# Second half's row sums by quarters, batched first norm, another order of the seven products, activation maximum in four parts

## The chip, the cores and the metric

One core of one Trainium2 chip runs the whole program in one launch. The metric is the device time of that core in microseconds (us); three runs of the kernel before took 2927.37, 2935.06 and 2939.93 us, median 2935.06.

## What is computed

One layer of a decoder trunk on x (1 x 2048 x 1024, float32). Cut to what matters:

```python
mod = silu(c) @ w_ada + b_ada;  sh1, sc1, g1, sh2, sc2, g2 = split(mod, 6)
h  = rms(x, ln1_g) * (1 + sc1) + sh1
u  = h @ w_in                       # q, k, v of 8 FoX heads and 4 differential heads
x  = x + g1 * (concat(fox(u), diff(u)) @ w_out)
h2 = rms(x, ln2_g) * (1 + sc2) + sh2
y  = (silu(h2 @ w_gate) * (h2 @ w_up)) @ w_down      # 1024 -> 2816 -> 1024
x  = x + g2 * y
```

## The kernel before

Every matmul operand is kept as two float16 parts, high and low, and each product is three matmuls (high x high, high x low, low x high). The 2048 rows are 16 blocks of 128.

The program has four stages. First the modulation and the first norm: `first_norm` squares a block on ScalarE with the row sum as accumulator output (L230), makes 1/sqrt with Ln, Exp and three small VectorE operations (`rsqrt`, L126 to L135), and scales the block on GpSimd (L235); `first_hT` turns it with PE transposes and splits it. `first_rows(c)` lists these steps for the four blocks of chunk c, and `run` mixes them by weights with the input projection of the chunk before. Then come the projection and attention of eight head groups. Then `out_proj(blk)` for the 16 blocks, which also stores the new x to `x1d` in DRAM and leaves 1/rms of each row in `r2`.

The last stage is the feed-forward part. It multiplies by a scheme of seven products in place of eight: the rows are taken in pairs of blocks (z) and the 1024 inputs in halves (h), and product i takes one combination of row quarters (`BSUM`), one combination of weight quarters (`ASUM`), and adds its result to the outputs. `norm_row` scales and shifts a row block (two VectorE operations over 1024 columns); `norm_sum` makes one combination (a GpSimd sum over 512 columns where two quarters are involved, a ScalarE copy to the high half, a VectorE subtraction to the low half), and transposes it by DMA. For the first half of the rows (pairs 0 to 3) this is done during the out projection, straight into `comb(i)`. For the second half (pairs 4 to 7) it is done inside the first pass, in iterations 2, 4, 6 and 8: `norm_load` takes two stage buffers for the two rows of a pair, each of the seven sums takes a third, and the transposed result goes to `hcd` in DRAM. There are three stage buffers in all (`stage`, tag S), shared with the down weights.

The loop has 22 iterations q and one more for the last downs: 11 weight chunks of 256 columns of the 2816, once for each half of the rows. An iteration has 14 slots: seven products in `ORDER` for the gate (w = 0), seven for the up weights (w = 1). `product(q, w, i)` is 12 matmuls of 512 columns into a bank of ps_st, ps_pv or ps_mx (2, 2 and 3 banks); products 2 and 3 add onto the banks of 4 and 5. What follows each product on the other engines makes `act`, four parts of 128 x 512, from sums of products, Silu for w = 0, the multiplication for w = 1. `act_scale(q)` takes the maximum over all of act (L123), spreads it over the partitions with a small matmul (`colmax`, L108, on the one bank of ps_ip), and makes a power of two from it; `act_split` then writes `aT`, and 16 `down` of six matmuls each, in the next iteration, multiply it by the down weights and are added to x on VectorE (L1153). Gate and up weights are loaded whole (`gu_load`, 1 MB), bounded by a maximum, summed on GpSimd (L1038) and split; the down weights are loaded, bounded (L1061, L1062) and split (`dn_load`, `dn_scale`, `dn_split`). Each of the four weight and activation maxima of an iteration goes through `colmax` and so puts one small matmul into PE's queue.

The order in which Python emits these steps is a priority; a planner with times of its own puts each engine's instructions into a fixed order from it, and inserts all semaphores. Every engine works its queue in order. All DMAs go over SP's queue. The list `st[slot]` says after which product a step is emitted, and `DOWNAT` how many downs follow each slot's product.

## Time and profile before

| | |
|---|---|
| runs | 2927.37, 2935.06, 2939.93 us |
| profiled execution | 2939.51 us, its span 2937.7 us |
| mean granted clock of TensorE | 0.980 |
| busy: PE, VectorE, ScalarE, GpSimd | 2728.9, 2111.3, 1441.2, 1609.5 us |
| stretch of the feed-forward part in the trace | about 1547 to 2937 us |

PE, DVE, ACT and POOL are TensorE, VectorE, ScalarE and GpSimd, SP is the queue that issues DMAs, L123 is line 123 of the kernel before. The granted clock is given as a share of 2.4 GHz. An idle time in square brackets is the time that the engine stood before that instruction, with what released it.

### The profile page before, as it was taken

The numbers are of one execution on the slowest core, as the hardware profiler recorded it, in microseconds if no ns is written. First come the engines' busy times: TensorE is split into PE (matmuls) and PEld (weight loads), VectorE is DVE, ScalarE is ACT, GpSimd is POOL, SyncE is SP. The second block draws the span as 40 slices with busy tenths as digits, with TensorE's granted clock in tenths as the row PEclk, the third lists the DMA queues.
The fourth block names the chain that finished last, engine by engine and source line by source line (L and its number), as shares of the span: only waits on it lengthen the run. The fifth ranks groups of instructions, "written<-read, shape, count | busy, mean of one in ns | idle before, by whom it ended". The sixth has DMA issues, their size and how long they took to land.

```text
span 2937.7 us, 49384 instructions
## 1 busy us (share of the span) xinstructions
PE 2728.9 (93%) x18902; PEld 1479.9 (50%) x18902; DVE 2111.3 (72%) x4077; ACT 1441.2 (49%) x2725; POOL 1609.5 (55%) x1392
## 2 busy tenths in 40 slices
PE   5789989899999999999989998899999999999998
PEld 3456656566665655664444343444444444444443
DVE  7786675857758686656744887787878778778775
ACT  4666667666676777786543422333323332233230
POOL 2566666665667787675542645444545444535430
PEclk9899999999999999999999999999999999999999
DMA  6232231322224233234776223224234511112101
GB/s 230 77 82 61 63 73 39 82 53 67 73 50 94 53 105 95 49 103 118 171 196 202 85 68 98 72 79 110 70 108 150 165 59 57 58 52 64 58 22 58
DMA packets 269902, 261.92 MB, mean 89 GB/s; under 512 B 204376, under 2 KB 221144, under 8 KB 263904
## 3 DMA queue, kind: packets, MB, share of 16 engines
q1 hardware_dynamic: 269664, 258.75, 31.0%
q8 instruction: 148, 2.42, 0.4%
q14 instruction: 90, 0.74, 0.1%
HBM read 173.55 MB, written 36.91 MB: 72 GB/s over the span
## 4 chain that ended last, share of the span: by engine, by line
PE 52%; DVE 21%; DMA 12%; POOL 6%; ACT 6%; issue 4%; SPq 0%; POOLq 0%; DVEq 0%; ACTq 0%
PE ps_mx L1149 10%; PE ps_ip L437 10%; PE ps_st L1091 7%; PE ps_pv L1091 6%; DMA stg<-in_w_ada_dram 3%; PE ps_ip L934 3%; DMA stg<-stg 2%; PE ps_mx L1091 2%; PE ps_st L579 2%; DVE t_mxc L548 2%; PE ps_st L580 2%; PE ps_pv L609 2%; PE ps_mx L546 2%; PE ps_pv L608 2%; PE ps_pv L607 2%
## 5 line engine op out<-in xcount | busy, mean ns | idle before, releaser
L593 POOL TENSOR_TENSOR pxs<-pxs 128x512 f16<-128x512 f32 (+3 forms) x640 | 683.3, 1082 | 325.8 <-ACT pxs L590 191.8
L1091 PEld LDWEIGHTS <-mt 128*128 128x128 f16 x3696 | 361.8, 99 | 446.7 <-issue 22.0
L437 PE MATMUL ps_ip<-wbuf,ht 128*128 128x384 f16 (+1 forms) x2952 | 560.6, 332 | 26.1 <-DVE vts L144 13.5
L1149 PE MATMUL ps_mx<-wide,ht 128*128 128x512 f16 x2112 | 505.4, 382 | 11.5 <-ACT ht L139 5.6
L1038 POOL TENSOR_TENSOR pxm<-vts 128x512 f32<-128x512 f32 x220 | 295.7, 1370 | 347.1 <-DMA vts<-in_w_gu_dram 316.3
L585 ACT ACTIVATE pxs<-ps_st,cells 128x512 f32<-128x512 f32 (+3 forms) x640 | 388.7, 619 | 142.5 <-PE ps_st L580 68.9
L437 PEld LDWEIGHTS <-ht 128*128 128x128 f16 x3072 | 295.7, 99 | 243.5 <-issue 46.2
L1091 PE MATMUL ps_st<-ht,mt 128*128 128x512 f16 x1584 | 383.0, 386 | 5.6 <-ACT mt L1094 3.2
L1091 PE MATMUL ps_pv<-ht,mt 128*128 128x512 f16 x1584 | 383.3, 380 | 1.1 <-ACT mt L1096 1.1
L590 ACT ACTIVATE pxs<-pxs 128x512 f16<-128x512 f32 (+3 forms) x640 | 350.7, 565 | 16.4 <-PE ps_pv L609 7.6
L607 PE MATMUL ps_pv<-vts,pxs 128*128 128x129 f16 (+1 forms) x2176 | 342.6, 207 | 4.2 <-DVE os L626 3.1
L608 PE MATMUL ps_pv<-vts,pxs 128*128 128x128 f16 (+1 forms) x2176 | 344.7, 208 | 0.0
L1149 PEld LDWEIGHTS <-ht 128*128 128x128 f16 x2112 | 206.3, 98 | 266.7 <-issue 16.9
L609 PE MATMUL ps_pv<-vts,pxs 128*128 128x129 f16 (+1 forms) x2176 | 325.6, 207 | 9.8 <-POOL pxs L593 8.9
L548 DVE TENSOR_REDUCE t_mxc<-ps_mx 128x1 f32<-128x512 f32 x384 | 256.9, 682 | 93.8 <-PE ps_mx L546 92.0
L1153 DVE SCALAR_TENSOR_TENSOR mt<-ps_mx,t_ai,mt 128x512 f32<-128x512 f32 x352 | 256.6, 743 | 75.5 <-PE ps_mx L1149 75.2
L607 PEld LDWEIGHTS <-pxs 128*128 128x128 f16 x2176 | 208.2, 97 | 56.7 <-ACT pxs L585 3.5
L579 PE MATMUL ps_st<-mt 67*128 67x512 f16 (+7 forms) x640 | 223.8, 350 | 10.4 <-ACT pxs L585 10.2
L609 PEld LDWEIGHTS <-pxs 128*128 128x128 f16 x2176 | 206.8, 99 | 50.0 <-POOL pxs L593 24.3
L608 PEld LDWEIGHTS <-pxs 128*128 128x128 f16 x2176 | 208.0, 97 | 35.3 <-issue 4.1
L580 PE MATMUL ps_st<-mt 128*128 128x512 f16 (+3 forms) x640 | 223.8, 350 | 0.0
L546 PE MATMUL ps_mx<-mt 71*128 71x512 f16 (+7 forms) x640 | 197.3, 350 | 19.6 <-DVE t_mxc L548 13.1
(266 smaller groups left out, 4097.0 us busy)
## 6 DMA issues: line engine op xcount, KB each, us to landing
vts<-in_w_gu_dram SPq DMA_DIRECT2D x44, 1024.0 KB
stg<-in_w_down_dram SPq DMA_DIRECT2D x44, 512.0 KB
stg<-in_w_ada_dram SPq DMA_DIRECT2D x32, 512.0 KB
stg<-in_w_in_dram SPq DMA_DIRECT2D x24, 512.0 KB
mt<-in_w_ada_dram SPq DMA_DIRECT2D x16, 512.0 KB
mt<-mt SPq DMA_DIRECT2D x128, 64.0 KB
mixed<-os SPq DMA_DIRECT2D x32, 256.0 KB
stg<-in_w_out_dram SPq DMA_DIRECT2D x16, 512.0 KB
```

The source lines that it names most:

```text
L437: T.matmul(pt[:, 0:N], lhsT=h4[:, k, hs, c : c + P], rhs=w4[k // 4][:, k % 4, ws, 0:N], start=(i == 0), stop=(i == len(terms) - 1))
L548: V.tensor_reduce(out=mx[:, 4 * j + n : 4 * j + n + 1], in_=b[:, 0:w], op=ALU.max, axis=AX.X)
L579: T.matmul(b[:, c0:QC], lhsT=K2[0:K, kb * P : (kb + 1) * P], rhs=QA[0:K, q0:q1], start=True, stop=False, skip_group_check=True)
L585: A.activation(p32[:, c0:QC], b[:, c0:QC], AF.Exp, bias=pshift, scale=1.0)
L590: A.activation(ph[:, c0:QC], p32[:, c0:QC], AF.Copy, bias=0.0, scale=1.0)
L593: (V if hilo[1] == "V" else G).tensor_tensor(out=pl[:, c0:QC], in0=p32[:, c0:QC], in1=ph[:, c0:QC], op=ALU.subtract)
L607: T.matmul(pv[:, jj, :], lhsT=lhs_h, rhs=v4[:, kb, h, 0 : W + 1], start=first, stop=False, skip_group_check=True)
L608: T.matmul(pv[:, jj, 0:W], lhsT=lhs_h, rhs=v4[:, kb, h, W + 2 : 2 * W + 2], start=False, stop=False, skip_group_check=True)
L609: T.matmul(pv[:, jj, :], lhsT=lhs_l, rhs=v4[:, kb, h, 0 : W + 1], start=False, stop=end, skip_group_check=True)
L1038: G.tensor_tensor(out=sums[:, k * 512 : (k + 1) * 512], in0=raw[:, a * 512 : (a + 1) * 512], in1=raw[:, b * 512 : (b + 1) * 512], op=op)
L1091: T.matmul(b.rearrange("p (b n) -> p b n", b=4), lhsT=aw[w][:, APOS[i] * 4 + k, ws, :], rhs=cb[:, :, 2 * k + hb, :], start=(fresh and k == ...
L1149: T.matmul(b, lhsT=aT[:, th, as_, f, j * P : (j + 1) * P], rhs=dnb[:, (2 * q + f) % 4, ws, n * 512 : (n + 1) * 512], start=(f == 0 and z = ...
```

## The change

It has four parts and two that come with them.

The second half's rows and sums become small units: `late_row` loads one block, scales and shifts it and stores it to a new DRAM tile `yd`; `late_sum` loads the one or two quarters that it needs from `yd` into one stage buffer, sums, splits, transposes and stores to `hcd`. Their steps have slots of their own; four units begin in every iteration from 0 to 8.

The first norm of chunks 1 to 3 squares the four blocks one after the other, makes one 1/sqrt of four columns, and scales each block.

The order of the products becomes 6, 4, 5, 1, 2, 3, 7. The sum of products 6 and 1 is made after product 1, and act[1,1] after product 3; after the last product only act[0,0] is left.

The maximum over act is taken in four parts of 512 columns, after the slots that make them, and `act_scale` reduces over the four.

With these, the down weights' steps move to the head of the iteration and the downs two slots later, and the first gate weights' steps are emitted between the out projections of blocks 10 to 13.

```diff
+    def first_stats(c, r4):
+        ss = small(4, "dss", bufs=2)
+        for j in range(4):
+            A.activation(sqs.bitcast(F16), xcs[c][:, j, :], AF.Square, bias=0.0, scale=1.0, accum_out=ss[:, j : j + 1])
+        V.tensor_scalar(out=ss, in0=ss, scalar1=1.0 / D, scalar2=EPS, op0=ALU.mult, op1=ALU.add)
+        r = small(4, "drr", bufs=2)
+        rsqrt(ss, r, 4)
+        r4["r"] = r
...
-        rows = [(0, lambda: hts.append(htile()))]
+        r4 = {}
+        rows = [(0, lambda: hts.append(htile())), (2, lambda: first_stats(c, r4))]
         for j in range(4 * c, 4 * c + 4):
-            rows.append((1, lambda j=j: first_norm(j)))
+            rows.append((0.5, lambda j=j: first_scale(j, r4)))
             rows.append((1, lambda j=j: first_hT(j)))
...
-    ORDER = (4, 5, 1, 2, 3, 7, 6)
+    ORDER = (6, 4, 5, 1, 2, 3, 7)
...
+    def late_row(blk):
+        st = {}
+        def load():
+            st["y"] = stage()
+            nc.sync.dma_start(st["y"], x1d[blk])
+        return [(0, load), (1, lambda: norm_rows2(st["y"], blk)), (2, lambda: nc.sync.dma_start(yd[blk - 8], st["y"]))]
+
+    def late_sum(jj, i):
+        (za, ha), op, other = BSUM[i]
+        st = {}
+        def load():
+            e = st["e"] = stage()
+            for c, (z, h) in enumerate([(za, ha)] + ([other] if other else [])):
+                nc.sync.dma_start(e[:, c * 512 : (c + 1) * 512], yd[2 * jj - 8 + z][:, h * 512 : (h + 1) * 512])
...
+        def add():
+            e = st["e"]
+            if other:
+                G.tensor_tensor(out=e[:, 0:512], in0=e[:, 0:512], in1=e[:, 512:1024], op=op)
+            s3, hi, _, _ = parts()
+            A.activation(hi, s3, AF.Copy, bias=0.0, scale=1.0)
+        def low():
+            s3, hi, lo, _ = parts()
+            V.tensor_tensor(out=lo, in0=s3, in1=hi, op=ALU.subtract)
...
+        return [(0, load), (1, add), (2, low), (3, turn), (4, store)]
...
         elif i == 1:
             V.tensor_tensor(out=tmp, in0=b, in1=s4s, op=ALU.add)
+            V.tensor_tensor(out=s5s, in0=e["b", w, 6], in1=tmp, op=ALU.add)
...
         elif i == 3:
             V.tensor_tensor(out=dif, in0=b, in1=dif, op=ALU.subtract)
+            G.tensor_tensor(out=s5s, in0=s5s, in1=dif, op=ALU.add)
             if w == 0:
                 A.activation(act[:, 1, 0], b, AF.Silu, bias=0.0, scale=gi)
+                A.activation(act[:, 1, 1], s5s, AF.Silu, bias=0.0, scale=gi)
             else:
                 V.tensor_tensor(out=act[:, 1, 0], in0=b, in1=act[:, 1, 0], op=ALU.mult)
+                G.tensor_tensor(out=act[:, 1, 1], in0=s5s, in1=act[:, 1, 1], op=ALU.mult)
         elif i == 7:
...
             V.tensor_tensor(out=tmp, in0=b, in1=tmp, op=ALU.add)
             if w == 0:
-                G.tensor_tensor(out=act[:, 1, 1], in0=tmp, in1=dif, op=ALU.add)
-                A.activation(act[:, 1, 1], act[:, 1, 1], AF.Silu, bias=0.0, scale=gi)
+                A.activation(act[:, 0, 0], tmp, AF.Silu, bias=0.0, scale=gi)
             else:
-                G.tensor_tensor(out=tmp, in0=tmp, in1=dif, op=ALU.add)
-                G.tensor_tensor(out=act[:, 1, 1], in0=tmp, in1=act[:, 1, 1], op=ALU.mult)
+                V.tensor_tensor(out=act[:, 0, 0], in0=tmp, in1=act[:, 0, 0], op=ALU.mult)
...
+    def act_bound(q, th, f):
+        e = sets[q]
+        if (th, f) == (0, 1):
+            e["am4"] = small(4, "am4", bufs=2)
+        k = 2 * th + f
+        V.tensor_reduce(out=e["am4"][:, k : k + 1], in_=act[:, th, f], op=ALU.max, axis=AX.X, apply_absolute_value=True)
...
-        g = colmax(absmax(uhm, BF16), "ip")
+        g = colmax(absmax(e["am4"], BF16), "ip")
...
+    run(outs[10:11])
     gu_bound(0, 0)
...
+    run(outs[11:13])
     gu_scale(0, 0)
+    run(outs[13:14])
...
-    run(outs[10:16])
+    run(outs[14:16])
...
-        return [(0, gu_load, q, 1), (1, gu_bound, q, 1)] + [(1 + k // 2, gu_sum, k) for k in range(5)] + [(2, gu_scale, q, 1)]
+        return [(0, gu_load, q, 1), (1, gu_bound, q, 1)] + [(1 + k // 2, gu_sum, k) for k in range(5)] + [(3, gu_scale, q, 1)]
...
-    DOWNAT = (0, 0, 0, 0, 2, 2, 2, 2, 2, 2, 1, 1, 1, 1)
+    DOWNAT = (0, 0, 0, 0, 0, 1, 2, 2, 2, 2, 2, 2, 2, 1)
...
+    seq = pairs[0] + pairs[1] + lates[0] + pairs[2] + lates[1] + pairs[3] + lates[2] + lates[3]
+    for k, steps in enumerate(seq):
+        for d, f in steps:
+            late[14 * (k // 4) + (5, 6, 10, 11)[k % 4] + d].append(f)
...
             for f in range(2):
-                at(3 + f, dn_load, q, f)
-            at(5, dn_scale, q)
+                at(f, dn_load, q, f)
+                at(1 + f, dn_bound, q, f)
+            at(3, dn_scale, q)
             for f in range(2):
-                at(9 + f, dn_split, q, f)
+                at(4 + f, dn_split, q, f)
+            for k, (th, f) in zip((12, 13, 13), ((0, 1), (1, 0), (1, 1))):
+                at(k, act_bound, q, th, f)
         if q:
-            at(0, act_scale, q - 1)
-            at(1, act_split, q - 1, 0)
-            at(2, act_split, q - 1, 1)
+            at(0, act_bound, q - 1, 0, 0)
+            at(1, act_scale, q - 1)
+            at(2, act_split, q - 1, 0)
+            at(3, act_split, q - 1, 1)
...
-            at(4, gu_scale, q + 1, 0)
+            at(5, gu_scale, q + 1, 0)
```

## Rows read from the trace of the kernel before

**Rows 1.** The page's first part: span; engine, busy us, share, instructions.

```profile
span 2937.7 us, 49384 instructions
PE 2728.9 (93%) x18902; PEld 1479.9 (50%) x18902; DVE 2111.3 (72%) x4077; ACT 1441.2 (49%) x2725; POOL 1609.5 (55%) x1392
```

**Rows 2.** Windows, both passes: stretch, length, PE, PEld, DVE, ACT, POOL busy, clock, DMA.

```profile
1651.00:2227.90 576.90, 534.10 (x2413) 236.98 (x2414) 457.59 (x644) 173.78 (x208) 297.33 (x188) 0.97 0.28 84
2402.80:2856.60 453.80, 453.80 (x2128) 206.40 (x2127) 357.67 (x529) 142.34 (x159) 206.08 (x138) 1.00 0.16 53
```

**Rows 3.** PE's waits, 1651 to 2227.9 us: us in total, times, longest.

```profile
PE ps_ip L108 <- DVE t_amh L123: 28.9, 6, 7.3
...
PE ps_mx L1149 <- DVE mt L1153: 3.0, 3, 2.1
```

**Rows 4.** PE in order of time around one stall: start us, us, instruction.

```profile
2017.17 2.75 PE L1091 MATMUL ps_mx<-ht,mt 128*128 128x512 f16 x12
...
2025.16 5.34 PE L1091 MATMUL ps_pv<-ht,mt 128*128 128x512 f16 x24
2036.48 0.29 PE L108 MATMUL ps_ip<-idb,t_amh 128*128 128x128 bf16 x1 [5.98 <-DVE t_amh L123]
2037.07 4.94 PE L1091 MATMUL ps_st<-ht,mt 128*128 128x512 f16 x12 [0.30 <-DVE pxm L1099]
```

**Rows 5.** VectorE in order of time, the same stall.

```profile
2034.13 2.29 DVE L123 TENSOR_REDUCE t_amh<-uhm 128x1 bf16<-128x2048 f32 x1 [3.59 <-POOL uhm L1126]
```

**Rows 6.** GpSimd in order of time, the same stall.

```profile
2027.49 1.27 POOL L984 TENSOR_TENSOR stg<-stg 128x512 f32<-128x512 f32 x1 [4.50 <-DMA hcd<-stg]
2028.72 1.27 POOL L1125 TENSOR_TENSOR pxm<-pxm,wide 128x512 f32<-128x512 f32 x1
2029.95 2.93 POOL L1038 TENSOR_TENSOR pxm<-vts 128x512 f32<-128x512 f32 x2
2032.85 1.25 POOL L1126 TENSOR_TENSOR uhm<-pxm,uhm 128x512 f32<-128x512 f32 x1
```

**Rows 7.** Window just after that stall, columns as in rows 2.

```profile
2036.80:2041.40 4.60, 4.33 (x11) 1.58 (x11) 3.96 (x6) 0.63 (x1) 0.29 (x1) 0.50 0.00 0
```

**Rows 8.** The last iteration's end, VectorE and PE in order of time.

```profile
2902.84 0.69 DVE L1120 TENSOR_TENSOR pxm<-ps_mx,pxm 128x512 f32<-128x512 f32 x1 [1.84 <-PE ps_mx L1091]
...
2908.59 0.29 PE L108 MATMUL ps_ip<-idb,t_amh 128*128 128x128 bf16 x1 [4.50 <-DVE t_amh L123]
```

**Rows 9.** Groups by line, 1651 to 2227.9 us: busy us, mean ns; idle before.

```profile
L984 POOL TENSOR_TENSOR stg<-stg 128x512 f32<-128x512 f32 x20 | 29.5, 1473 | 103.3 <-DMA hcd<-stg 101.0 <-DVE wide L144 2.4
L989 DVE TENSOR_TENSOR stg<-stg 128x512 f16<-128x512 f32 x28 | 24.6, 880 | 44.5 <-ACT stg L988 44.5
...
L974 DVE SCALAR_TENSOR_TENSOR stg<-stg,cells,vts 128x1024 f32<-128x1024 f32 x8 | 15.4, 1930 | 0.0
L975 DVE TENSOR_TENSOR stg<-stg,vts 128x1024 f32<-128x1024 f32 x8 | 12.8, 1594 | 0.0
```

**Rows 10.** VectorE's reduction over 512 columns, line 455: ns min/median/max.

```profile
L455 DVE TENSOR_REDUCE t_ss<-os x64: 668/676/689, 63.9 to 1331.6; 128x8 f32<-128x512 f32 x64
```

**Rows 11.** PE at the end of the out projection, in order of time.

```profile
1539.86 0.29 PE L108 MATMUL ps_ip<-idb,t_amh 128*128 128x128 bf16 x1 [7.37 <-DVE t_amh L123]
1540.53 6.64 PE L934 MATMUL ps_ip<-mt,wide 128*128 128x512 f16 x24 [0.38 <-DVE t_cm L109]
```

**Rows 12.** PE's waits, 2227.9 to 2860 us.

```profile
PE ps_ip L108 <- DVE t_amh L123: 3.5, 1, 3.5
```

**Rows 13.** First norm: groups by line, ScalarE and VectorE, 40 to 440 us.

```profile
L230 ACT ACTIVATE os<-mt 128x1024 f16<-128x1024 f32 x12 | 12.7, 1055 | 3.2 <-DVE t_ss L455 3.2
...
L230 ACT ACTIVATION_READ_ACCUMULATOR os<-mt 128x1 f32 x12 | 2.3, 188 | 0.0
```

**Rows 14.** VectorE's split by form, second pass, 2402.8 to 2856.6 us.

```profile
L144 DVE SCALAR_TENSOR_TENSOR wide<-stg,t_dws,wide 128x1024 f16<-128x1024 f32 x16 | 29.1, 1856 | 3.9 <-ACT wide L139 3.9
...
L144 DVE SCALAR_TENSOR_TENSOR mt<-vts,t_ws,mt 128x1024 f16<-128x1024 f32 x16 | 20.5, 1283 | 4.0 <-ACT mt L139 3.1
```

More of the change, by code (lines that the diff above doesn't have):

```diff
@@ L292, in first_norm, with first_scale @@
         norm_rows(xt, xt)
+    def first_stats(c, r4):
[6 more added lines that the diff above has]
+        r4["r"] = r
+    def first_scale(blk, r4):
+        xt = xcs[blk // 4][:, blk % 4, :]
+        G.tensor_scalar(out=xt, in0=xt, scalar1=r4["r"][:, blk % 4 : blk % 4 + 1], scalar2=0.0, op0=ALU.mult, op1=ALU.add)
     def first_hT(blk):
@@ L909, in trunk @@
     hcd = dram.tile([7, 4, P, 1024], F16, tag="hcd", name="hcd")
+    yd = dram.tile([8, P, D], F32, tag="yd", name="yd")
     hs = []
@@ L989, in norm_sum, with parts, turn, store @@
         V.tensor_tensor(out=hl[:, :, 1, :], in0=s3, in1=hl[:, :, 0, :], op=ALU.subtract)
-        row = hl.rearrange("p k s n -> p (k s n)")
-        if jj < 4:
-            nc.sync.dma_start(comb(i)[:, jj], row, transpose=True)
-        else:
-            tr = e[:, 0:512].bitcast(F16)
-            nc.sync.dma_start(tr.rearrange("p (k n) -> p k n", n=P), row, transpose=True)
-            nc.sync.dma_start(hcd[ORDER.index(i), jj - 4], tr)
+        nc.sync.dma_start(comb(i)[:, jj], hl.rearrange("p k s n -> p (k s n)"), transpose=True)
+    def late_row(blk):
[11 more added lines that the diff above has]
+                nc.sync.dma_start(e[:, c * 512 : (c + 1) * 512], yd[2 * jj - 8 + z][:, h * 512 : (h + 1) * 512])
+        def parts():
+            e = st["e"]
+            hl = e[:, 512:1024].bitcast(F16).rearrange("p (k s n) -> p k s n", k=4, s=2)
+            return e[:, 0:512].rearrange("p (k n) -> p k n", k=4), hl[:, :, 0, :], hl[:, :, 1, :], hl.rearrange("p k s n -> p (k s n)")
+        def add():
+            e = st["e"]
+            if other:
[5 more added lines that the diff above has]
+            V.tensor_tensor(out=lo, in0=s3, in1=hi, op=ALU.subtract)
+        def turn():
+            tr = st["e"][:, 0:512].bitcast(F16)
+            nc.sync.dma_start(tr.rearrange("p (k n) -> p k n", n=P), parts()[3], transpose=True)
+        def store():
+            nc.sync.dma_start(hcd[ORDER.index(i), jj - 4], st["e"][:, 0:512].bitcast(F16))
+        return [(0, load), (1, add), (2, low), (3, turn), (4, store)]
     def norm_pair(jj):
@@ L1191, in trunk @@
         f(*a)
+    late = [[] for _ in range(14 * (NQP + 1))]
+    pairs = [[late_row(2 * jj + z) for z in range(2)] for jj in range(4, 8)]
+    lates = [[late_sum(jj, i) for i in ORDER] for jj in range(4, 8)]
+    seq = pairs[0] + pairs[1] + lates[0] + pairs[2] + lates[1] + pairs[3] + lates[2] + lates[3]
+    for k, steps in enumerate(seq):
+        for d, f in steps:
+            late[14 * (k // 4) + (5, 6, 10, 11)[k % 4] + d].append(f)
     for q in range(NQP + 1):
@@ L1219, in trunk @@
                 at(9 + k, f, *a)
-        if q in (2, 4, 6, 8):
-            jj = 4 + q // 2 - 1
-            for z in range(2):
-                at(8, norm_load, jj, z)
-                at(9 + z, norm_row, jj, z)
-            for k, i in enumerate(ORDER):
-                at(min(13, 10 + k // 2), norm_sum, jj, i)
         nd = 0
@@ L1238, in trunk @@
                     nd += 1
-            for f in st[slot]:
+            for f in late[14 * q + slot] + st[slot]:
                 f()
```

23 lines of the change are left out of this document (6 added, 17 removed).

## The prediction

> **What bounds the kernel now.** I read the windows first, the way a table by stage is read, then PE's waits in the stretches where PE is not full, then the timelines of the engine that ended the longest wait.
>
> The span is 2937.7 us with PE busy for 93% of it [rows 1], so only stretches where PE idles or runs slow can give time. The feed-forward part runs 22 iterations; I mark the end of one by the matmul of the activation's column maximum (L108 on ps_ip, wait on t_amh). Nine periods of the first pass (iterations 1 to 9) take 576.9 us, 64.1 each, eight of the second pass 453.8 us, 56.7 each, for the same matmuls [rows 2]. In the second pass PE is busy all the time at full clock: 56.7 is the floor. In the first pass it idles 576.9 - 534.1 = 42.8 us and the mean granted clock is 0.97. The excess is 9 x 7.4 = 66 us.
>
> 28.9 of the idle 42.8 us are one wait: the column-maximum matmul stands in PE's in-order queue and its input is late [rows 3]. The stall at 2030.5 shows why. The iteration's last product ends at 2019.9, PE runs 10.6 us of the next iteration's products ahead, then stands 5.98 us before the small matmul [rows 4]. Its input is the reduction over all of act, 2.29 us, which waited for POOL [rows 5]. On POOL the two operations that make act[1,1] stand behind L984, a row sum of the second half, which had itself waited 4.50 us until a stage buffer was stored and free, and behind two weight sums [rows 6]. After the stall the clock is granted at 0.50, which is the 1.2 of the two levels 1.2 and 2.4 GHz, and 12 matmuls take 4.94 us [rows 4, 7]. The six waits cost 28.9 us, and a long one about half of 4.6 us of slow clock besides [rows 3, 7].
>
> **The change part by part.**
>
> *Act maximum in four parts, other order of products.* Today the chain behind the last product (6) is: VectorE add 0.69, two POOL adds or products of 1.27 and 1.25 at best, reduction 2.29 [rows 5, 6, 8]. Afterwards the last product is 7, and behind it stand a VectorE add (0.69), a VectorE product of two SBUF operands (the nearest row is L989, mean 0.88, down to about 0.7), a reduction over 512 columns (0.68) and one over four values: 2.4 us and nothing on POOL [rows 8, 9, 10]. act[1,1] is made after product 3, with two downs, product 7 and one more down behind it in program order: 2 x 1.3 + 2.6 + 1.3 = 6.5 us of PE work, taking a matmul of 512 columns at 5.34/24 = 0.22 us [rows 4]. Its chain (0.69 + 1.27 + 1.25 + 0.68 = 3.9) fits with 2.6 to spare. The present delay on POOL is 11 us: from the last product's end at 2019.9 to L1125 at 2028.7, less the VectorE add, 8.1, plus 2.9 between the two POOL operations [rows 4, 6]. If it stayed, 11 - 2.6 less the two products (5.2) that stand ahead of the small matmul in program order would leave 3 us of stall. A caution belongs here: the planner puts the small matmul where its own times expect it ready, so a shorter chain also moves the matmul forward. What goes is the part that the planner did not foresee, the wait for buffers on POOL.
>
> *Row sums by quarters.* Before, 28 sums and 8 row norms sit in four of the iterations, each holding two or three of the three stage buffers. After, 36 units, four per iteration in nine iterations, hold one buffer each. Work per unit stays: POOL sum 1.47, copy, VectorE 0.88, transpose, store; per row 1.93 + 1.59 on VectorE [rows 9]. New are 8 stores to yd and 48 loads of half a row block. They go over SP: 56 more issues in nine periods, 6 per period, each behind the units' own waits. Nothing on PE reads them before iteration 11, so their latency is free; the danger is that SP, in order, holds back the gate/up or down weights. VectorE's load is the tighter point: the late work is 8 x 3.52 + 28 x 0.88 = 53 us, 5.9 a period when spread evenly, and the other edits add 3 reductions' overhead and one product, about 1.4 us. 50.8 (457.6/9) + 1.4 = 52.2 us of a 56.7 us period [rows 2, 9]: 92%. It fits, with little room. What remains per period: today's idle other than the 28.9 is 13.9 us, 1.5 a period, and I leave 1.0 for maxima still late. 56.7 + 2.5 = 59.2. Bounds: 56.7 (all gone, -66 us) and 64.1 (none, 0), above that only by the rivals below. Value: 9 x (59.2 - 64.1) = **-44**.
>
> *Out projection of block 10 ahead of the first weight bound.* PE stands 7.37 us at 1532.5 behind the first iteration's small matmul, while 24 matmuls of the out projection are queued right behind it, and these then take 6.64 us where 24 take 5.34 at full clock [rows 4, 11]. Afterwards they come first in program order. Bounds 0 and -8.7 (7.4 and 1.3 of slow clock); value **-6**.
>
> *Rest of the stage.* One stall between the passes, 3.5 us [rows 12], with the same releaser: value -3.5 (0 to -5). The end of iteration 0: -2 (0 to -4). The tail: PE waits 4.50 us for the last maximum, of which 2.29 are the full reduction [rows 5, 8]; the new chain is 2.4, so -2 (0 to -4). Behind it act_split is unchanged.
>
> *First norm by fours.* It removes nine chains of Ln, Exp and five small VectorE operations, and adds a wait: the first scale of a chunk stands behind four squares (1.055 + 0.188 each) instead of one, 3.7 us per chunk, 11 us for three chunks if nothing hid it; the removed ones, seven a chain at about the 0.188 of the accumulator read, make 12 us [rows 13]. The chunk is prepared while the one before is projected, which covers it, and other queues end most waits there. Value 0, bounds -12 and +11.
>
> *Moved down-weight load, bound, scale and split.* Two loads, two reductions of VectorE, two POOL products and the splits now stand at the head of the iteration instead of its middle, in SP's queue ahead of the next gate load; they are used only in the next iteration: 0. If the stage buffer comes late, the dn maximum can stand in PE's queue as the act maximum does now; that is inside the 1.0 above.
>
> *Product 6 first.* Its ps_mx bank is now held from product 6 until the sum after product 1, four products, instead of one drain. In the second half of an iteration eight downs share two banks. The present wait for a down's drain is 3.0 us in three waits, with three banks [rows 3]. Value **+2** for both passes, bounds 0 and +84 (rival 2).
>
> Sum: -44 - 6 - 3.5 - 2 - 2 + 2 = -55.5. The profiled execution took 2939.5 us (1.8 around its span), so 2884; it was 4.5 above the median of 2935.1, from which the same difference gives **2880**, my forecast for the median, with an own range of 2858 to 2902.
>
> **One rule that speaks against it.** VectorE's form of L144 with stage operands takes 1856 ns in the second pass where the same shape from vts takes 1283 [rows 14]: it is lengthened when POOL works beside it. The Trainium skill, "SBUF — State Buffer" (SBUF: two separate sides), says why: a VectorE operation with two SBUF inputs and a GpSimd operation take one port pair by an exclusive lock, and the loser is blocked for the whole instruction. The change moves one such product to VectorE and lets sums fall beside VectorE's work in every iteration. The trace agrees with the rule as far as these two rows go; by the rule the added product would cost up to 0.69 + 1.27 instead of 0.88, which would be rival 1 in one more place; its price below is from rows alone.
>
> **The rivals.**
>
> 1. *VectorE takes the place of POOL.* At 92% with lengthened operations and waits for new loads standing in its queue, the period would still hang on what VectorE ends last. For it: in the first pass L974 and L975 take 1.93 and 1.59, L989 0.88 where 0.69 is the least [rows 8, 9]; if the ten or so two-operand operations of a period are lengthened by 0.5 us each (the two forms of L144 lie 0.57 apart [rows 14]), VectorE has 52.2 + 5 = 57 us, more than the 56.7. With small waits around it the period is about 62, so 9 x -2.1 = -19, and the other parts at half value, -5: **2911**. Against it: the late sums are lengthened already in the 50.8. Chance 0.18.
>
> 2. *Slower: two banks for the downs.* If VectorE, now nearer to full, drains a down later than the 3.9 us that another down and a product give it, PE waits at L1149. With four such waits an iteration of 1.0 us, the present mean, 21 iterations lose 84 us in both passes, and 84 - 55 gives **2964**. For it: VectorE's single operations of up to 2.3 us stand ahead of a drain [rows 5]. Against: in the second pass no PE wait is seen at all [rows 2, 12], and the planner can put matmuls of a product ahead of a down. It decides from 2.6 us lost per iteration upwards. Chance 0.10.
>
> 3. *The maximum is as late as before*, since the units' loads, through DRAM now, keep POOL waiting, and PE's order follows the planner's optimistic times: only block 10 and the tail gain, less the bank waits, 6 + 2 - 2: **2929**. For it: POOL waited for DMA-freed buffers at each of these sums [rows 6, 9]. Chance 0.08.
>
> The forecast has 0.64. Within 0.5% of the median means 2920 to 2950, about what a measurement of this kernel can tell from no change. Faster by more: 0.64 + 0.14 of rival 1 = 0.78; within: 0.04 + 0.08 = 0.12; slower: 0.10. The range reaches from the best of the forecast to rival 3: 2856 to 2936.
>
> **What would show it.** Right: first-pass periods of 58 to 60 us, the L108 wait on act gone or below 8 us in total, no half clock after iteration ends, reductions of 0.68 us in place of 2.29, second pass still at 56.7. Wrong: waits of L1149 on ps_mx for VectorE in both passes (rival 2), VectorE over 93% in the first pass with periods above 61 (rival 1), or POOL's row sums still waiting several us for DMA with the small matmul behind them (rival 3).

## The result, and the profile after

The changed kernel takes 2960.65 us (median of 4 runs, 2959.32 to 2974.94) against 2931.22 us (4 runs) for the kernel before on the same chip: ratio 1.0107, 95% interval 1.009 to 1.0125. It is 1.1% slower; 2880 was forecast.

The page's first part and the two windows of the kernel after, cut at the same matmul of the activation maximum as [rows 1, 2]; columns as there:

```profile
span 2959.8 us, 49574 instructions
PE 2740.6 (93%) x18902; PEld 1483.8 (50%) x18902; DVE 2145.5 (72%) x4151; ACT 1434.1 (48%) x2704; POOL 1566.5 (53%) x1370
```

```profile
1663.30:2243.30 580.00, 531.94 (x2400) 235.13 (x2401) 454.62 (x677) 173.87 (x209) 270.57 (x177) 0.98 0.34 104
2418.00:2878.90 460.90, 460.90 (x2161) 210.05 (x2160) 366.45 (x568) 142.09 (x160) 188.60 (x132) 1.00 0.16 52
```

The first window is no shorter (576.9 before), VectorE in it no fuller (457.6 before), GpSimd 27 us emptier, and the DMAs move 104 GB/s instead of 84. PE's waits in that window, the kernel after (us in total, times, longest):

```profile
PE ps_mx L1202 <- DVE mt L1206: 29.7, 20, 4.3
PE ps_ip L108 <- DVE t_cm L109: 6.4, 3, 2.3
PE ps_mx L1142 <- DVE mt L1206: 4.4, 6, 2.1
PE ps_mx L1202 <- DVE mt L1151: 3.9, 3, 3.3
PE ps_ip L108 <- DVE t_amh L123: 1.6, 2, 1.4
```

The wait for the maximum, 28.9 us in [rows 3], is 1.6. In its place stands a wait of nearly the same size, of the downs (L1202) for VectorE's drain (L1206, the add to x that frees a down's bank), 3.0 us in [rows 3]. PE's waits behind that window, to 2881 us, all of them:

```profile
PE ps_mx L1202 <- ACT ht L139: 2.6, 1, 2.6
PE ps_mx L1202 <- DVE mt L1206: 2.0, 2, 1.3
```

The last maximum's matmul, for which PE stood 4.50 us in [rows 8]:

```profile
2930.04 0.23 PE L108 MATMUL ps_ip<-idb,t_amh 128*128 128x128 bf16 x1 [1.67 <-DVE t_amh L123]
```

Since the order of PE's queue changed, windows between equal events hold unequal work. So I count matmuls: the time at which the n-th matmul of out projection, products and downs starts, less n x 0.2155 us (their pitch where PE is full). By how much this grows is the time lost there:

| stretch | before | after |
|---|---|---|
| start of the out projection (us) | 1345.8 | 1348.8 |
| lost in matmuls 1 to 768 (out projection) | 82.9 | 89.9 |
| lost in 769 to 3672 (first pass) | 70.3 | 83.1 |
| lost in 3673 to 6576 (second pass, tail) | 17.6 | 16.6 |

The 22.1 us between the two spans are 3.0 + 7.0 + 12.8 - 1.0, and 0.3 of rest. The medians lie 29.4 apart: the profiled execution of the kernel before, 2939.51 us, was one of its longest.

One stall of the kernel after, on SP, VectorE and PE in order of time (start, length, instruction, idle before it). L1019, L1039 and L1042 are load, transpose and store of a late sum, L1108 and L1112 load and maximum of the down weights, L1079 the load of the gate or up weights; in some runs below these numbers are one less.

```profile
1987.17 1.24 SPq L1039 DMA_TRANSPOSE stg<-stg  x1
1990.23 0.33 SPq L1042 DMA_DIRECT2D hcd<-stg  x1
1992.54 0.33 SPq L1108 DMA_DIRECT2D stg<-in_w_down_dram  x1
```

```profile
1989.77 0.15 DVE L123 TENSOR_REDUCE t_amh<-t_dam 128x1 bf16<-128x2 f32 x1
1996.31 1.22 DVE L1112 TENSOR_REDUCE t_dam<-stg 128x1 f32<-128x1024 f32 x1 [6.40 <-DMA stg<-in_w_down_dram]
1997.45 0.28 DVE L109 TENSOR_REDUCE t_cm<-ps_ip 128x1 f32<-128x128 f32 x1
```

```profile
1997.79 0.22 PE L108 MATMUL ps_ip<-idb,t_amh 128*128 128x128 bf16 x1 [2.25 <-DVE t_cm L109]
```

SP transposes a late sum, waits for it, stores it, and only then issues the down weights; VectorE stands 6.40 us at their maximum, everything behind it in its queue is late, and PE waits. SP's last 2.0 us ahead of the load are for the landing of that store, which frees the load's stage buffer, so this event holds both SP's order and the buffer. It is one event; the runs below show how much each weighs.

### The profile page after: what moved, and what is told of

It reads as the page before. It is cut to its first block, busy times and chain, and to the rows that moved or that the text cites. A ratio compares the mean times of both kernels' runs of the same rounds, so it can differ in the third digit from the quotient of the medians.

```text
span 2959.8 us, 49574 instructions
## 1 busy us (share of the span) xinstructions
PE 2740.6 (93%) x18902; PEld 1483.8 (50%) x18902; DVE 2145.5 (72%) x4151; ACT 1434.1 (48%) x2704; POOL 1566.5 (53%) x1370
## 5 line engine op out<-in xcount | busy, mean ns | idle before, releaser
L1202 PE MATMUL ps_mx<-wide,ht 128*128 128x512 f16 x2112 | 507.7, 385 | 43.5 <-DVE mt L1206 31.8
L1202 PEld LDWEIGHTS <-ht 128*128 128x128 f16 x2112 | 207.5, 99 | 304.9 <-issue 54.3
L1206 DVE SCALAR_TENSOR_TENSOR mt<-ps_mx,t_ai,mt 128x512 f32<-128x512 f32 x352 | 258.4, 743 | 50.7 <-PE ps_mx L1202 50.1
L623 PEld LDWEIGHTS <-pxs 128*128 128x128 f16 x2176 | 207.1, 99 | 49.7 <-POOL pxs L607 22.1
L560 PE MATMUL ps_mx<-mt 71*128 71x512 f16 (+7 forms) x640 | 197.5, 350 | 18.3 <-DVE t_mxc L562 13.8
```

What stands on the lines that cost most here:

```text
L623: T.matmul(pv[:, jj, :], lhsT=lhs_l, rhs=v4[:, kb, h, 0 : W + 1], start=False, stop=end, skip_group_check=True)
L1202: T.matmul(b, lhsT=aT[:, th, as_, f, j * P : (j + 1) * P], rhs=dnb[:, (2 * q + f) % 4, ws, n * 512 : (n + 1) * 512], start=(f == 0 and z = ...
L1206: V.scalar_tensor_tensor(out=xs, in0=b, scalar=sets[q]["ai"], in1=xs, op0=ALU.mult, op1=ALU.add)
```

## The experiments

"Rows alone", "no late work" and the like are kernels in which part of the work is missing, as each expectation says. Each entry ends with its median, its ratio to the kernel before on the same chip and the loss in the first pass (70.3 before, 83.1 after). The loss is read from one execution of each. A cost given below is a difference of two medians, mostly from different chips; taken against the kernel before on each chip it comes out up to 5 us otherwise. The planner orders every one of these kernels anew, so a part that is left out also moves what stays, except where the text says that the order is the same.

**1. First weights' steps emitted ahead of out projections 10 to 15 again.**

```diff
-    run(outs[10:11])
     gu_bound(0, 0)
...
-    run(outs[14:16])
+    run(outs[10:16])
```

> The kernel after, with the first gate weights' steps (load, bound, sums, scale, split) all emitted ahead of the out projections 10 to 15 again. In the kernel after the first product of the feed-forward part starts at 1604 us, after the last out projection, where before it had started at 1547, and down 0 comes 13.3 us later than before. Theory EMISSION: this is because the weights' bound and splits were emitted behind out projections, so no product could fill out projection's gaps. Then products run from about 1550 on again, down 0 returns by 10 to 13 us, the first pass (down 0 to down 10: 632 us after, 625 before) stays, and the time is 2946 to 2952 against 2961. Rival ORDER: the delay comes from product 6 being first, which needs the second split and the last part of the transposed sums: down 0 stays within 3 us of the kernel after's, time 2957 to 2963.

2960.19 us, 1.0095 (1.0065 to 1.0125); loss 88.8. Products do start at 1551.6 instead of 1604.2, but the out projection then ends at 1610.8 instead of 1604.4 and down 0 comes at 1677.8 (1675.6). EMISSION names what moved the start and is worth nothing. The rival's numbers came true; its cause, product 6, was not tried.

**2. Product 6's bank freed at once.**

```diff
+        if i == 6:
+            A.activation(dif, b, AF.Copy, bias=0.0, scale=1.0)
...
-            V.tensor_tensor(out=s5s, in0=e["b", w, 6], in1=tmp, op=ALU.add)
+            V.tensor_tensor(out=s5s, in0=dif, in1=tmp, op=ALU.add)
```

> The kernel after, with product 6 copied out of its bank by ScalarE at once (into dif, which is free then); the sum with product 1 reads the copy. So the three ps_mx banks serve the downs as before. In the kernel after PE waits 29.7 us in 20 waits of the first pass for a down's drain, 4.4 us where a product 6 waits for a bank, and 3.9 us where a down waits for the sum that frees product 6's bank. Theory BANK: the held bank is the cause. Then these waits fall from 38 to under 12 us, the first pass from 632 to 600 to 612 us, and the time to 2932 to 2944. Rival QUEUE: VectorE comes late to a drain because late sums and weight maxima that wait for DMA and ScalarE stand ahead of it; a third bank helps by less than half: waits 20 to 35 us, time 2948 to 2962. ScalarE gets 44 copies of about 0.7 us, which lie beside PE's work in either theory.

2971.93 us, 1.0134 (1.0103 to 1.0164); loss 89.1. PE still waits 26.8 us for drains in the first pass, in 11 waits instead of 20. BANK falls: with three banks the drains' waits are nearly as long.

**3. Low part of the late sums on GpSimd.**

```diff
-            V.tensor_tensor(out=lo, in0=s3, in1=hi, op=ALU.subtract)
+            G.tensor_tensor(out=lo, in0=s3, in1=hi, op=ALU.subtract)
```

> The kernel after, with the low part of the 28 late sums subtracted on GpSimd instead of VectorE, so that VectorE's queue no longer stands at that subtraction for ScalarE (51 us in 15 waits of the first pass). Theory QUEUE: PE's waits for the drain fall from 29.7 to under 12 us and the time by 15 to 25 us, to 2936 to 2946, unless GpSimd (46% busy) makes act late again. Theory BANK: PE's waits for the drain fall by less than a third, since VectorE's other waits (for down weights 24 us, for GpSimd 18 us) still exceed what two banks cover; time 2952 to 2962.

2962.54 us, 1.0103 (1.0077 to 1.0128); loss 87.6. Drain waits fall to 15.9 us, but product 6's wait for a bank rises from 4.4 to 14.4, and VectorE, no longer behind ScalarE, stands 47.0 us behind GpSimd (L1150) where it stood 18.4. Neither theory's numbers came: taking out one link moves the wait to the next.

**4. Late work in the old form.** `late_row` and `late_sum` replaced by `norm_load`, `norm_row`, `norm_sum` of the kernel before, in iterations 2, 4, 6 and 8.

> The kernel after, with the second half's rows and sums made as before the change (pairs of rows in stage buffers in iterations 2, 4, 6 and 8); everything else as after. Theory QUEUE: without units spread over every iteration VectorE waits little, and PE's waits for drains occur in the four iterations with row sums only: under 12 us in the first pass; waits for act's maximum come back in those iterations only as far as act[1,1]'s two GpSimd steps are late, 0 to 15 us; time 2935 to 2952. Theory BANK: with two banks the drains are waited for 20 us or more whatever the form of the late work, and with the blocks of sums in four iterations more than that there; time 2955 to 2975.

2937.19 us, 1.0023 (1.0006 to 1.004); loss 65.5. The form of the late work is worth 23 us: that is most of the slowdown. Drain waits are 21.3 us with it, so the number that I had expected to tell the theories apart didn't; run 7 does.

**5. Old form, and the first weights' steps as in 1.**

> Two edits undone: late rows and sums as before, and the first gate weights' steps ahead of out projections 10 to 15. The first alone gave 2937 us. With the weights' steps alone undone, products filled out projection's gaps from 1551 us on, but the first iterations lost it again, with late units in them. Theory CHAIN (each late unit is a chain SP, DMA, POOL, ACT, VectorE, SP, DMA, whose links the engines wait for in their queues, from iteration 0 on): without the units in iterations 0 and 1 the emission's gain stays, 8 to 14 us: 2923 to 2930. Rival ORDER: with product 6 first the products ahead are worth nothing in iteration 0 whatever the late work: 2934 to 2940.

2936.78 us, 1.0011 (0.9998 to 1.0023); loss 61.8, out projection 91.1. Again nothing from the emission, as the rival had it. All other edits together are thus worth nothing that this interval shows.

**6. As 5, with product 6's bank freed as in 2.**

> As the kernel with late work and first weights' steps undone, and product 6 copied out of its bank by ScalarE at once, so that the downs have three banks. With late work as before, PE still waited 21.3 us for drains, 6.2 us for a bank at product 6 and 4.5 us for the sum that frees it in the first pass. Theory BANK (now that VectorE is not held by late units): these 32 us fall below 12 and the time is 12 to 20 us under the same kernel without the copy. Rival: with late units, the copy left 26.8 us of drain waits and gained nothing; if VectorE's lateness comes from its other links (sums on POOL, down weights from DMA), waits stay at 20 to 30 us and the time within 5 us of the kernel without the copy.

2943.88 us, 1.0036 (1.002 to 1.0051); loss 65.5. Drain waits are 16.2 us (18.6 in run 5), product 6's wait for a bank 3.0 (6.9). It is seven us slower than 5, two more than the rival allowed: nearer the rival than BANK, and the copies cost something.

**7. As 1, no late work at all.**

```diff
-            late[14 * (k // 4) + (5, 6, 10, 11)[k % 4] + d].append(f)
+            pass
```

> The kernel after with the first weights' steps ahead of out projections 10 to 15 and without the second half's rows and sums: late_row and late_sum are left out, and the second pass multiplies by the first half's sums. It measures what all late work costs on top of the order, bank and maximum edits. Theory CHAIN: the late units are what the first pass loses; without them its periods are 57 to 59 us, drain waits under 8 us, time 2890 to 2905. Theory BANK: two banks cost 15 us or more in drain waits of the first pass without any late work too; periods 59 to 61, time 2905 to 2925.

2876.02 us, 0.9809 (0.9792 to 0.9825); loss 11.8. PE's waits from 1640 to 2300 us, all of them:

```profile
PE ps_mx L1202 <- DVE mt L1206: 2.9, 1, 2.9
PE ps_mx L1202 <- ACT ht L139: 2.1, 2, 1.5
PE ps_mx L1202 <- DVE ht L144: 0.6, 1, 0.6
```

With two banks for the downs and no late work there is one drain wait. The time is below both expectations. Late work costs 82 us after (2958, run 8, to 2876).

**8. As 1, one slot more between a late sum's load and its add.**

> The kernel after with the first weights' steps ahead of out projections 10 to 15, and one more slot between a late sum's load and its add; the later steps move along by one slot. Theory CHAIN with the load as its worst link (GpSimd stands 65 us at the add for loads from yd that were issued some 3 us before): the DMA wait at the add falls below 25 us, PE's drain waits below 15 us, time 2930 to 2945. If the chain's links are late because each unit's load waits for the buffer that the unit before stores from, one slot changes where they stand and not how long: 2953 to 2965.

2957.94 us, 1.0088 (1.0073 to 1.0103); loss 87.5. GpSimd stands 80.0 us at the add. Emitting later only moves where the chain waits.

**9. The kernel before without its late work.**

> The kernel before without norm_load, norm_row and norm_sum of the second half (the second pass multiplies by the first half's sums). The kernel after without its late units took 2876 us against 2958 with them (first weights' steps undone in both): its late work costs 82 us, while the same kernel with late work in the old form took 2937, a cost of 61. Theory LATE: all of the difference between before and after is the form of the late work; the order, the bank, the maxima in parts, the down weights' place and the first norm come to nothing: 2866 to 2882 here. Rival ORDER: these edits cost something of their own, which shows without late work: under 2862. If they gain (the chain of act is shorter): over 2886.

2874.9 us, 0.9802 (0.9777 to 0.9826); loss 14.8. LATE holds: without late work both kernels take the same time, and the whole difference is 82 us against 58 for it. By stretches the other edits do not vanish but cancel: run 7 loses 88.8 us in the out projection, 11.8 in the first pass and 14.4 behind it, this one 80.9, 14.8 and 17.0.

**10. As 1, late sums from constant columns instead of loads.**

```diff
-                nc.sync.dma_start(e[:, c * 512 : (c + 1) * 512], yd[2 * jj - 8 + z][:, h * 512 : (h + 1) * 512])
...
-                G.tensor_tensor(out=e[:, 0:512], in0=e[:, 0:512], in1=e[:, 512:1024], op=op)
+                G.tensor_tensor(out=e[:, 0:512], in0=mod[:, 0:512], in1=mod[:, 512:1024], op=op)
```

> The kernel after with the first weights' steps undone (2958 to 2960 us) and with the late sums' loads from yd left out: each sum is made from constant columns in SBUF, so that its GpSimd, ScalarE and VectorE work, its transpose and its store stay. Theory CHAIN with the load as its worst link: GpSimd's 80 us at the add for yd go, VectorE's 55 us behind ScalarE's copy fall below 25, PE's drain waits below 12; 2915 to 2935. Rival CAPACITY: VectorE's added work and the buffers' turn by transpose and store are what counts, loads are not: 2945 to 2958.

2943.66 us, 1.0027 (1.0008 to 1.0046); loss 70.7. The 48 new loads carry 14 of the 21 us between the two forms (2958 and 2937, runs 8 and 5; by the ratios 18 of 23); drain waits stay at 19.6. Between my two expectations.

**11. As 1, late rows alone.**

> The kernel after with the first weights' steps undone and the 28 late sums left out; the eight late rows (a load, two VectorE operations of 1024 columns, a store each, in iterations 0, 1, 3 and 5) stay. By their work on VectorE, 28 of 53 us, the rows would carry half of the late cost of 82 us: CAPACITY expects 2905 to 2925. CHAIN expects little of them, since one link of a row unit waits for its load and nothing stands behind its store: 2880 to 2895.

2888.86 us, 0.9855 (0.9823 to 0.9886); loss 24.1. Rows cost 13 us, the 28 sums about 69.

**12. Rows, and the sums' engine work without any DMA.**

```diff
-        return [(0, load), (1, add), (2, low), (3, turn), (4, store)]
+        return [(0, load), (1, add), (2, low)]
```

> First weights' steps undone; the late sums keep only their work on engines (add on GpSimd, copy on ScalarE, low part on VectorE, from constant columns), without load, transpose and store; the second pass multiplies by the first half's sums; the late rows stay whole. With everything the kernel takes 2958, with rows alone 2889, without the loads 2944. Theory CHAIN (what costs is that the links wait for DMAs and for the buffer that the store frees, with other work queued behind): 2889 to 2903. Rival CAPACITY (28 x 0.9 us of VectorE's time and 20 x 1.3 of GpSimd's delay drains by themselves): 2918 to 2940.

2899.32 us, 0.9896 (0.9879 to 0.9914); loss 33.8. All the sums' work on three engines costs 10 us: CAPACITY falls.

**13. Rows, and the sums' DMAs without engine work.**

```diff
-        return [(0, load), (1, add), (2, low), (3, turn), (4, store)]
+        return [(0, load), (3, turn), (4, store)]
```

> The counterpart: first weights' steps undone; the late sums keep only their DMAs (two loads from yd, a transpose of a block of the first half's sums, the store), without add, copy and low part; the second pass multiplies by the first half's sums; the late rows stay whole. Theory CHAIN holds that engines stand for DMAs that they need; with no engine step between them the sums' DMAs hurt only through SP's queue, where weight loads stand behind them: 2889 to 2905. Rival SP-QUEUE (the weights come late because SP works the units in order): 2915 to 2945.

2943.98 us, 1.005 (1.0035 to 1.0065); loss 74.8. I had thought the engine links essential; they aren't: the DMAs alone cost 55 us. (Every sum has two loads here, 56 in place of 48.) What waits on SP from 1640 to 2300 us, first in run 11, then here:

```profile
SPq L1079 <- DVE mt L144: 299.0, 21, 27.9
SPq L1108 <- DVE wide L144: 154.4, 13, 22.3
SPq L1108 <- DVE t_cm L109: 66.0, 3, 22.0
```

```profile
SPq L1108 <- DVE wide L144: 134.4, 9, 24.3
SPq L1079 <- DVE mt L144: 127.0, 12, 28.0
SPq L1108 <- DVE t_cm L109: 87.3, 4, 22.3
SPq L1039 <- DMA stg<-yd: 61.6, 27, 5.1
SPq L1042 <- DMA stg<-ht: 54.8, 27, 4.6
SPq L1019 <- DMA hcd<-stg: 33.3, 20, 2.7
...
SPq L1108 <- DMA hcd<-stg: 13.9, 7, 3.8
```

With rows alone SP stands ready 299 us at the gate or up load (L1079) until its buffer is free, 21 times: such a load leaves at once. With the sums' DMAs SP stands 150 us for one of them after the other, and is early at L1079 only 12 times. At the down weights' load (L1108) it is early by about as many us as before, but 13 times instead of 16, and 7 times it waits there for a sum's store to free the stage buffer, 13.9 us. VectorE's waits for weights, first in run 11, then here:

```profile
DVE t_dam L1112 <- DMA stg<-in_w_down_dram: 9.1, 11, 2.2
DVE t_amh L123 <- DMA vts<-in_w_gu_dram: 6.6, 5, 1.5
```

```profile
DVE t_dam L1112 <- DMA stg<-in_w_down_dram: 49.9, 16, 10.5
DVE t_amh L123 <- DMA vts<-in_w_gu_dram: 23.2, 10, 5.4
```

**14. As 1, gate and up weights from GpSimd's queue.** `nc.sync` replaced by `nc.gpsimd` in `gu_load`.

> First weights' steps undone, and the gate and up weights loaded from GpSimd's queue instead of SP's. In the kernel after SP stands 99 us in the first pass at these loads, whose buffer is not yet free, with late units' loads queued behind. If that order makes the yd loads late, GpSimd's wait for them (80 us) halves and the time falls by 8 to 20 us from 2958, unless GpSimd, which now stands at the loads itself, delays its sums: then 2955 to 2975.

2955.98 us, 1.0093 (1.0067 to 1.0119); loss 81.7. GpSimd's wait for yd halves (46.1), it stands 33.5 us at the loads instead, and VectorE waits 22.7 us for down weights. No gain.

**15. As 5, the high half copied on VectorE.** `V.tensor_copy` in place of `A.activation` for the second half's sums.

> Late work in the old form and first weights' steps undone (2937 us), and the high half of the 28 late sums copied on VectorE instead of ScalarE. VectorE stood 69 us in 20 waits for that copy in the first pass, ScalarE before it 94 us for GpSimd's sum, GpSimd 74 us for a stage buffer to be stored. Theory CHAIN: the wait only moves to GpSimd's sum; 2930 to 2942. If ScalarE's own queue made the copies late, VectorE's wait falls below 40 us and the time to 2918 to 2930.

2952.43 us, 1.0075 (1.0058 to 1.0093); loss 72.7. VectorE stands 48.6 us for GpSimd's sum and 14.4 for the store. Worse than either expectation.

**16. SP's order alone: tiny DMAs, no stage buffer, no engine work.**

```diff
-            e = st["e"] = stage()
+            e = st["e"] = wide[:, 4608:4672]
...
-        return [(0, load), (1, add), (2, low), (3, turn), (4, store)]
+        return [(0, load), (3, turn), (4, store)]
```

> First weights' steps undone; the late sums keep only the order of their DMAs on SP, with all waits of one for the other (two loads, a transpose, the store), but with 64 columns in a small buffer of their own in place of a stage buffer, so that hardly a byte moves and no stage buffer is held; no engine step, and the second pass multiplies by the first half's sums; the late rows stay whole. Rows alone gave 2889, whole DMAs 2944. Theory SP-QUEUE (weight loads stand in SP's queue behind the units' waits for each other): 2920 to 2945. Rival BUFFERS (a down weight waits for a stage buffer that a unit holds): 2889 to 2905. A load lands as long after its issue with the units' DMAs as without (1 MB 5.0 and 5.3 us, 0.5 MB 3.5 and 3.6 us), so transfers in each other's way are expected to be worth little.

2927.59 us, 0.9994 (0.9977 to 1.0011); loss 53.5. Of the 55 us of run 13, 39 remain with hardly a byte moved and no stage buffer held. The four engines work the same instructions in the same order as in run 11, but for 27 of 4123 places on VectorE, one on PE and one on ScalarE; so no new order of the planner is in the 39 us. (Run 13 differs from run 11 in 1045 of PE's 18902 places; its other 16 us hold bytes, buffers and order.) VectorE's waits for weights are 19.5 + 17.6 us. One stall of this run, on SP, VectorE and PE:

```profile
1917.46 1.10 SPq L1038 DMA_TRANSPOSE wide<-ht  x1
...
1924.85 2.42 SPq L1019 DMA_DIRECT2D wide<-yd  x4
1928.62 1.10 SPq L1038 DMA_TRANSPOSE wide<-ht  x1
1930.83 0.33 SPq L1041 DMA_DIRECT2D hcd<-wide  x1
1932.30 1.10 SPq L1038 DMA_TRANSPOSE wide<-ht  x1
1934.51 0.33 SPq L1041 DMA_DIRECT2D hcd<-wide  x1
1934.88 0.91 SPq L1107 DMA_DIRECT2D stg<-in_w_down_dram  x2
```

```profile
1929.92 0.14 DVE L115 TENSOR_SCALAR t_p2a<-t_cm 128x1 f32<-128x1 f32 x1
1938.69 1.22 DVE L1111 TENSOR_REDUCE t_dam<-stg 128x1 f32<-128x1024 f32 x1 [8.63 <-DMA stg<-in_w_down_dram]
...
1939.94 0.74 DVE L1205 SCALAR_TENSOR_TENSOR mt<-ps_mx,t_ai,mt 128x512 f32<-128x512 f32 x1
```

```profile
1940.74 2.72 PE L1201 MATMUL ps_mx<-wide,ht 128*128 128x512 f16 x6 [8.52 <-DVE t_gi L119]
```

Two tiny units stand ahead of the down weights' loads, and from 1925 us to these loads SP waits for nothing but the units' own DMAs. VectorE waits 8.63 us for the weights, with a drain (L1205) behind, and PE waits 8.52 us (put down to t_gi, the small operation next to that drain). The six matmuls that follow take 2.72 us at a granted clock of 0.50 (1940.7 to 1943.3 us); twelve at full clock take 2.75 in [rows 4].

**17. As 1, the late sums' DMAs from ScalarE's queue.** `nc.sync` replaced by `nc.scalar` in `late_sum`.

> The kernel after with the first weights' steps undone, and the DMAs of the late sums (loads, transposes, stores) issued from ScalarE's queue instead of SP's; rows stay on SP. Theory SP-QUEUE: the weights come on time (VectorE's waits for down weights fall from 21 to under 12 us); if ScalarE, 30% busy, can stand some 150 us for the units without delaying its copies and splits, the time falls by 15 to 40 us from 2958; if these delays reach PE instead (its waits for ScalarE's halves and banks rise), 2955 to 2990. Rival BUFFERS: weights come no earlier, 2955 to 2990.

2943.47 us, 1.0043 (1.0028 to 1.0058); loss 71.7. VectorE's wait for down weights falls from 20.8 to 11.8 us and 14.5 us come back, a little under what was expected; drains are still waited for 24.3 us, now with ScalarE's copies (45.0) ahead. SP itself now stands 127 us at the down weights' loads for stage buffers that sums hold, in 16 waits (11.6 us in run 8).

**18. The kernel before with the same change of queue** for the transposes and stores of its late sums.

> The kernel before with the transposes and stores of the second half's sums issued from ScalarE's queue instead of SP's; nothing else. In the form of after, taking the units off SP's queue gave 14.5 us of the 82 that late work costs there. Theory SP-QUEUE: the late work's 58 us in the kernel before hang on SP's order too; 8 to 18 us faster, 2912 to 2924, faster than both kernels. Rival: in the old form the sums have one stage buffer, each waits for the store of the one before whatever queue issues it, and ScalarE now stands for its own stores: 2928 to 2940.

2942.46 us, 1.0055 (1.0038 to 1.0072); loss 78.9. Slower by more than the rival allowed: what helps the new form harms the old one. GpSimd still waits 53.5 us for the store of the sum before (101.0 before), VectorE's wait for down weights falls from 12.6 to 6.3, and ScalarE stands 20.2 us for its own transposes; that this last is what costs 13 us is not shown. No complete version that I ran beats the kernel before.

## Why the prediction was wrong, point by point

- **What bounds the first pass.** The excess was read rightly and placed rightly: without late work the loss there falls from 70.3 to 14.8 us (run 9). But I took the stalls at one reader, the maximum, for the thing to remove. They are where lateness came out, not where it arose. A sign stood in [rows 9]: GpSimd waited 101.0 us for the stores of late sums, a chain through DMA that the change kept.
- **Act maximum in four parts.** Right in itself: the wait fell from 28.9 to 1.6 us, a part takes 0.68 us as forecast, the tail's stall went from 4.50 [rows 8] to 1.67 us. It gave little to the sum (with the other edits and late work in the old form the first pass loses 61.8 to 65.5, runs 4 and 5, 70.3 before): PE, no longer held at the maximum, waits at the drains instead (21.3 us in run 4).
- **Row sums by quarters: the step that failed.** "Nothing on PE reads them before iteration 11, so their latency is free; the danger is that SP, in order, holds back the gate/up or down weights." The danger was named and priced at nothing. It is the largest single cost that the runs isolate: 39 us for SP's order alone (run 16), 55 with bytes and buffers (13), 13 for the rows (11), 10 for the engines' work (12), 82 with all, against 58 for the old form. So the -44 is + 12.8. The old form also sends its sums over SP's queue, and its 58 us were not taken apart: of the 24 us between the forms the new loads carry 14 to 18, and the rest is not told apart.
- **Block 10 ahead of the first bound, -6.** The 7.37 us gap of [rows 11] is gone, and the stage lost 7.0 us more. PE's waits in the out projection's own matmuls, 1282 to 1604 us, rose from 11.9 to 18.3 us (for drains and for transposed rows). Run 1 shows that the emission isn't why: with it undone the loss is 88.9. All kernels with the change's other edits lose 87 to 93 us there, the three of the old kind 81 to 83. Which edit does it wasn't tried.
- **Rest of the stage, end of iteration 0, tail: -7.5.** Second pass and tail gained 1.0 together. The tail did what was forecast: the 102 matmuls behind the last product lose 6.7 us instead of 9.2. The rest of the second pass lost 1.5 more than before; the 3.5 us of [rows 12] are gone, and the two waits shown above, 2.6 and 2.0 us, stand there now.
- **First norm, moved down steps: 0.** The out projection starts at 1339 to 1352 us in the traces with the new norm and at 1338 to 1346 in those with the old; nothing can be told from that. Runs 7 and 9 leave no room for a cost of more than a few us, unless another edit gave it back.
- **Product 6 first, +2.** Its bank costs next to nothing without late work (2.9 us of drain waits, run 7), and a third bank, bought with a copy on ScalarE, gained nothing (runs 2 and 6).
- **Rival 2** named the wait that came, L1149 (now L1202) for VectorE, but for the bank and in both passes; the second pass has 2.0 us of it. Its 2964 lies near the measured time by luck, since the bank is not the cause. **Rival 1** is out: VectorE was busy 454.6 us, not more than before. **Rival 3** is out: the maximum is not late. Its condition came true all the same: GpSimd waits 66.6 us for the loads from yd (14 waits, 1640 to 2300 us), but the small matmul no longer stands behind it. The missing rival was SP's queue.

The kernel after, VectorE and GpSimd:

```profile
1687.86 3.00 DVE L144 SCALAR_TENSOR_TENSOR mt<-vts,t_ws,mt 128x1024 f16<-128x1024 f32 x1
```

```profile
1687.42 2.37 POOL L1113 TENSOR_TENSOR stg<-stg,grep 128x1024 f32<-128x1024 f32 x1 [2.71 <-DVE t_dam L1112]
```

A split takes 3.00 us here where 1.27 is the least, while GpSimd works beside it. That agrees with the rule of the Trainium skill's page "SBUF — State Buffer" (section "SBUF: two separate sides") that the prediction weighed, by which a VectorE operation with two SBUF inputs and a GpSimd operation exclude each other. It is no part of the difference: in the first window VectorE is busy 454.6 us with 677 instructions, 457.6 with 644 before.

From issue to a reader that waited for it a 1 MB load of gate or up weights takes 5.0 us (medians worked out from the traces) in runs 11 and 16, 5.3 in run 13, 5.5 in the kernel after. So loads were late mainly because they were issued late. Another statement of the Trainium skill's page "SBUF — State Buffer" (section "SBUF: two separate sides") bears on this: engine ports and DMA ports cannot contend, so a DMA is not slowed by an engine's work. The traces agree: run 12 adds the sums' engine work and none of their DMAs to run 11, and the load takes 5.1 us there instead of 5.0.

## What to carry to other kernels

Price a DMA that "nobody waits for" by what stands behind it on its queue: here a load, transpose and store that depend on each other kept SP standing for each landing, and loads that were needed in time paid for it. Before removing a wait, ask whether it is the cause or only the first reader of a lateness; a kernel with the suspected work left out asks that in one run, and here run 9 would have shown that late work cost 58 us where the wait at the maximum was 28.9. And count lost time per matmul, not per window, where the order of the queue changed.

## What the runs showed that I had not expected

A chain of small DMAs costs the issuing queue about 70% of what one of full size does. In run 16 two units with their loads hold SP for 11.2 us (from the transpose at 1917.46 to that at 1928.62), 5.6 each; in run 13 a unit holds it for about 8 us:

```profile
1941.12 1.55 SPq L1039 DMA_TRANSPOSE stg<-ht  x1
1944.19 0.33 SPq L1042 DMA_DIRECT2D hcd<-stg  x1
1946.25 0.80 SPq L1019 DMA_DIRECT2D stg<-yd  x2
1949.09 1.24 SPq L1039 DMA_TRANSPOSE stg<-ht  x1
```

The store follows the issue of the transpose by 3.1 us there, by 2.2 in run 16. Moving the sums' DMAs to another engine's queue gave 14.5 us in one form of the kernel; moving their transposes and stores took 13 in the other. And among the kernels with the new norm the out projection, after the same steps in the program, began between 1339 and 1352 us in different traces, which is more than any of the small terms of my sum; one trace of each doesn't tell whether the kernel or the execution does it.
